# Feed-forward over quarters: the element-wise sums moved from GpSimd to VectorE, and the second product's sums read from PSUM

## The chip, the core and the metric

One core of one Trainium2 chip runs the whole program. The metric is the device time in microseconds of one execution; lower is better. The times shown are those of three runs, and one more execution was profiled.

## What is computed

One layer of a diffusion backbone over 1024 tokens of width 1024: four parallel token mixers, their gated sum and an output projection, then a feed-forward part, then a last RMSNorm. All in float32. The part that matters here is the feed-forward part and the norms around it:

```
bl = modulate(rms_norm(hl, norm_g[i, 1]), ml[3], ml[4])
hl = hl + ml[5] * (jnp.square(jax.nn.relu(bl @ w_ff1[i])) @ w_ff2[i])
return rms_norm(hl, final_g)
```

`w_ff1` is 1024 x 4096 and `w_ff2` is 4096 x 1024.

## The kernel before

The mixers take the first 948 us of the profiled execution; nothing in them is touched. The feed-forward part follows, and its order is written out by hand (`tc.manual_schedule()`): within one engine the instructions run in the order in which the Python loop emits them.

**The products.** Each of the two big products is cut into quarters (two halves of the tokens, `T1s` and `T2s`, by two halves of the contraction), and each 2 x 2 block product is made with seven products of sums and differences of quarters in place of eight products. There are 32 visits, `u` = 0 to 31: 16 for the first product, 16 for the second. A visit has seven steps, `j` = 0 to 6, so there are 224 steps. A step (`product`, lines 1469 to 1487) multiplies a 128 x 512 weight tile by one of seven stored operands `xo[j]`. Every float32 operand is held as a high part in FP32R and a low remainder, so a step is 4 x 3 = 12 matmuls of 128x512: high by high, high by low, low by high (lines 1485 to 1487). They accumulate in the PSUM banks `X`, `Y` and `Z` of the visit; the running sums of the seven-product scheme are partly made by going on accumulating in a bank after an intermediate value was read from it. Visits 0 to 9 (`PRO`) make their steps 0 and 1 first, 20 steps ahead, while the operands `xo[2]` to `xo[6]` of the second token half are still being prepared by `second_half` (lines 1619 to 1691). Visits 10 to 15 run alone; visits 16 to 31 run in pairs, step by step in turn; visits 28 to 31 make their steps 3 and 5 at the very end.

**The weights' side.** `fetch` loads four 128 x 512 quarters per visit by DMA on SP's queue, nine steps ahead at most. `weight_sum` (line 1438) makes four sums or differences of them per visit on GpSimd (line 1443), mostly in place. `prep_hi` (ScalarE, line 1461) and `prep_lo` (VectorE, through the helper `tt`, line 65) make the high part `ah` and the low part `al` of a step's weights two steps ahead; there are three buffers of each.

**After a step.** In round `n` of the main loop (from line 1900 on) these are emitted in turn: the matmuls of step `n`; `after1` or `after2` for the result of step `n - 1`; `prep_hi(n + 2)`; what was deferred to round `n` in `todo` (the weight sums among it); `prep_lo(n + 2)`; a piece of `second_half`; the fetches; and the refills.

- `after1` (line 1707), first product: ScalarE or VectorE reads the bank, the four values h11, h12, h21, h22 of the hidden layer are made, relu-squared, and turned into seven combinations. Four differences, of which two (`t3`, `t1`) go through `padd` (line 1704, GpSimd, line 1705), and the sum for h22 too. Each combination is written to DRAM (`hop`, line 1702).
- `after2` (line 1777), second product: a value is added into the residual `hl` in SBUF either by `whole`, one VectorE instruction that reads PSUM, scales and adds (line 72), or by `part`: ScalarE copies and scales the bank into an SBUF tile `m` (line 1785), and GpSimd adds `m` to `hl` a round later (line 1705).

**The refills.** The hidden combinations are the operands of the second product: from visit 15 on, the tiles `xo[j]` are loaded again from `hop`, 28 refills for each of four blocks of the contraction. A refill is a DMA load on SP's queue (line 1893), a high part on ScalarE (line 1614) and a low part on VectorE (line 1618). The main loop issues `pace` of them per round: 1.8 in the rounds before 125 and 1.35 later (line 1954). A refill's high and low parts follow its load by about four refills.

**The end.** `norm_part` squares and scales the finished pieces of `hl`, and `last_norm` totals them and scales the output (line 1869: seven instructions on VectorE and GpSimd, three of them here on GpSimd), which SP's queue stores.

Of the kernel before, what the change touches and what calls it, by code (L numbers as in the profile page):

```python
# [53 lines left out]
def tile_backbone(ctx: ExitStack, tc: tile.TileContext, a: dict, out: bass.AP):  # L54
# [9 lines left out]
    def tt(o, x, y, op):  # L64
        V.tensor_tensor(out=o, in0=x, in1=y, op=op)  # L65
# [1372 lines left out]
    def weight_sum(v, what):  # L1438

        q = v["q"]  # L1440

        def add(o, x, y, op=ALU.subtract):
            G.tensor_tensor(out=o, in0=x, in1=y, op=op)  # L1443

        if what == 4:
            q["s3"] = t_("s3", 2, where=hp)
            add(q["s3"], q[0, 0], q[1, 0])
        elif what == 3:
            add(q[1, 0], q[1, 0], q[1, 1], ALU.add)
        elif what == 2:  # L1450
            add(q[0, 0], q[1, 0], q[0, 0])
        else:
            add(q[0, 1], q[0, 1], q[0, 0])
# [156 lines left out]
    def mtile():  # L1610
        return t_("m", 4)
# [1 line left out]
    def operand_hi(j, k, src):  # L1613
        S.activation(xo[j][0][:, k], src, AF.Copy)  # L1614

    def operand_lo(j, k, src, eng=None):
        xh, xl = xo[j]
        (eng or V).tensor_tensor(out=xl[:, k], in0=src, in1=xh[:, k].bitcast(F32), op=ALU.subtract)  # L1618

    def second_half():  # L1620

        hl = box["hl"]
        y = finish_rstd(hp, box["ss"][:, :4], 4, "rf")
        dgs = hid()
        for t in range(4):
            ts(dgs[:, t * 128 : (t + 1) * 128], ident, y[:, t : t + 1], ALU.mult)
        bd = hp.tile([128, 4], F32, name="bd")
        tt(bd, modl[1][:, 4:8], modl[1][:, 0:4], ALU.subtract)
        yield
        rb = ps_n()  # L1630
        for t in range(4):
            T.matmul(rb[:, t * 128 : (t + 1) * 128], ones, dgs[:, t * 128 : (t + 1) * 128], start=True, stop=True)
        yield
        t1, t2, t3 = {}, {}, {}

        def v(k, half):
            return hl[:, k, T2s if half else T1s]

        def b2(k):
            return modl[1][:, k + 4 : k + 5]  # L1640


        def st0(k):
            second_scale(v(k, 1), k, rb)
            second_scale(v(k + 4, 1), k + 4, rb)
            t1[k] = hid()
            G.tensor_tensor(out=t1[k], in0=v(k, 1), in1=v(k, 0), op=ALU.subtract)

        def st1(k):
            second_hi(v(k + 4, 1), k + 4, xo[5])  # L1650

        def st2(k):
            operand_hi(3, k, t1[k])
            second_lo(v(k + 4, 1), k + 4, xo[5])
            t2[k] = hid()
            stt(t2[k], v(k + 4, 1), b2(k), t1[k], ALU.add, ALU.subtract)

        def st3(k):
            operand_hi(2, k, t2[k])
            operand_lo(3, k, t1[k], G)  # L1660

        def st4(k):
            operand_lo(2, k, t2[k])

            stt(t2[k], v(k + 4, 0), b2(k), t2[k], ALU.add, ALU.subtract)

        def st5(k):
            operand_hi(6, k, t2[k])

        def st6(k):  # L1670
            operand_lo(6, k, t2[k], G)

        def st7(k):
            t3[k] = hid()
            stt(t3[k], v(k + 4, 1), bd[:, k : k + 1], v(k, 1), ALU.add, ALU.subtract)

        def st8(k):
            operand_hi(4, k, t3[k])

        def st9(k):  # L1680
            operand_lo(4, k, t3[k])

        plan = {}
        for k in range(4):
            for m, f in enumerate((st0, st1, st2, st3, st4, st5, st6)):
                plan.setdefault(2 * k + m, []).append((f, k))
            for m, f in enumerate((st7, st8, st9)):
                plan.setdefault(11 + k + m, []).append((f, k))
        for n in sorted(plan):
            for f, k in reversed(plan[n]):  # L1690
                f(k)
            yield
# [8 lines left out]
    def save(j, u, x):  # L1701
        nc.sync.dma_start(hopd[j][u], x)

    def padd(o, x, y, op=ALU.add):
        G.tensor_tensor(out=o, in0=x, in1=y, op=op)  # L1705

    def after1(n, u, j, c, pro):

        if j == 0:
            c["m1"] = mtile()  # L1710
            S.activation(c["m1"], c["Z" if pro else "X"], AF.Copy)  # L1711
            if pro:
                nc.sync.dma_start(m1d[u], c["m1"])
        elif j == 1:
            h = c["h11"] = hid()
            if pro:
                square(h, c["Z"])
            else:
                tt(h, c["Z"], c["m1"], ALU.add)
                if u == 15:  # L1720
                    defer(n + 1, lambda: (square(h, h), save(0, u, h)))
                    return
                square_v(h)
            save(0, u, h)
        elif j in (2, 4):
            m = c["u2" if j == 2 else "u3"] = mtile()
            if pro:
                tt(m, c["X"], c["m1"], ALU.add)
            else:
                S.activation(m, c["X"], AF.Copy)  # L1730
            if j == 4:
                c["h22"] = hid()
                defer(n, lambda: padd(c["h22"], m, c["m5"]))
                defer(n + 1, lambda: (square(c["h22"], c["h22"]), save(5, u, c["h22"])))
        elif j == 3:
            c["m5"] = mtile()
            S.activation(c["m5"], c["Y"], AF.Copy)
            if pro:
                c["h11"] = hid()
                nc.sync.dma_start(c["h11"], hopd[0][u])  # L1740
        elif j == 5:
            h = c["h12"] = hid()
            tt(h, c["Y"], c["u2"], ALU.add)
            if pro or u == 15:
                defer(n + 1, lambda: square(h, h))
            else:
                square_v(h)

            def t3():
                t = hid()  # L1750
                padd(t, c["h22"], h, ALU.subtract)
                save(4, u, t)

            def t1():
                padd(h, h, c["h11"], ALU.subtract)
                save(3, u, h)

            def t2():
                tt(c["h22"], c["h22"], h, ALU.subtract)
                save(2, u, c["h22"])  # L1760

            def t4():
                tt(c["h21"], c["h21"], c["h22"], ALU.subtract)
                save(6, u, c["h21"])

            for k, f in enumerate((t3, t1, t2, t4)):
                defer(n + 1 + (pro or u == 15) + k, f)
        else:
            h = c["h21"] = hid()
            if pro:  # L1770
                tt(h, c["X"], c["m1"], ALU.add)
                defer(n + 1, lambda: (square(h, h), save(1, u, h)))
            else:
                square(h, c["X"])
                save(1, u, h)

    def after2(n, u, j, c):

        d = 2 * (u % 4)
        s1, s2 = modl[3][:, d : d + 1], modl[3][:, d + 1 : d + 2]  # L1780
        o11, o12, o21, o22 = (box["hl"][:, e, xs] for e in (d, d + 1) for xs in (T1s, T2s))

        def part(bank, s, o):
            m = mtile()
            S.activation(m, bank, AF.Copy, scale=s)  # L1785
            defer(n + 1, lambda: padd(o, o, m))

        def whole(bank, s, o):
            stt(o, bank, s, o, ALU.mult, ALU.add)

        last = u >= 28
        if j == 0:
            part(c["X"], s1, o11)
        elif j == 1:
            whole(c["Z"], s1, o11)
            if last:
                defer(n + 2, lambda: norm_part(n + 2, d, 0))
        elif j == 2:
            part(c["X"], s1, o12)
        elif j == 3:  # L1800
            if last:
                whole(c["Y"], s2, o22)
                norm_part(n, d + 1, 1)
            else:
                part(c["Y"], s2, o22)
        elif j == 4:
            part(c["X"], s2, o22)
        elif j == 5:
            whole(c["Y"], s1, o12)
            if last:  # L1810
                norm_part(n, d, 1)
        else:
            whole(c["X"], s2, o21)
            if last:
                norm_part(n, d + 1, 0)

    done_parts = [0, 0]
    N = len(steps)
# [90 lines left out]
    for n in range(N + 1):  # L1909
# [41 lines left out]
            S.activation(one, onec, AF.Sqrt)  # L1951
        fetch(n)
        if queue or waiting:
            pace += 1.8 if n < 125 else 1.35
            while pace >= 1.0:
                pace -= 1.0
                x = waiting.pop(0) if len(waiting) > 3 or (waiting and not queue) else None
                if queue:
                    waiting.append(queue.pop(0))
                    waiting[-1][0]()  # L1960
                if x:
                    x[1]()
                    x[2]()
                    fresh[x[3]] = (x[4], fresh[x[3]][1] + 1 if fresh[x[3]][0] == x[4] else 1)
# [84 lines left out]
```

## Time and profile before

| | us |
|---|---|
| three runs | 1612.93, 1618.04, 1617.37 |
| their median | 1617.37 |
| the profiled execution, its own time | 1611.68 |
| its span, first to last instruction | 1609.9 |
| TensorE busy in it | 1552.7 |
| VectorE busy | 1122.0 |
| ScalarE busy | 692.2 |
| GpSimd busy | 563.5 |
| first matmul of the feed-forward part starts at | 948.27 |
| last matmul of it starts at | 1588.94 |

PE is TensorE, DVE VectorE, ACT ScalarE, POOL GpSimd, SP the engine whose queue issues the DMAs. A busy time counts an instruction from its start to its end; neighbours in a pipeline overlap, so busy times can add up to a little more than the time that passed, and a 128x512 matmul of 392 ns does not mean one matmul every 392 ns. `al<-q,ah` reads: tile `al` is written from `q` and `ah`. `xl` and `xh` are the low and high parts of `xo[j]`, `m` an evacuated bank, `mm` a PSUM bank, `t` a tile of the hidden layer, `s` and `q` weight quarters.

### The profile page before, as it was taken

Reading aid. Unit: us, or ns where it says so; the run is one execution under the profiler, and the core shown is the slowest. Engines: PE = TensorE matmul, PEld = TensorE weight load, DVE = VectorE, ACT = ScalarE, POOL = GpSimd, SP = SyncE. Lnnn points to the kernel's source line nnn. Section 1 sums busy time; section 2 is a strip of 40 time slices with the busy share of each in tenths; the row PEclk is TensorE's granted clock in tenths of the full one; section 3 lists DMA queues with packets and bytes.
Section 4 is the critical chain, followed back from the end, with each engine's and each line's share of the span. In section 5 each row is a group of like instructions: output and inputs, shape, how many; then the busy total and the mean of one; then the engine's idle time right before and its main releaser. Section 6 shows DMA issues by size and latency. Waiting matters only on the chain.

```text
span 1609.9 us, 22494 instructions
## 1 busy us (share of the span) xinstructions
PE 1552.7 (96%) x8032; PEld 1277.1 (79%) x8032; DVE 1122.0 (70%) x2011; ACT 692.2 (43%) x1183; POOL 563.5 (35%) x515
## 2 busy tenths in 40 slices
PE   7999999999999999999999998999999889999996
PEld 6888878888788787778888886788888677878875
DVE  5797877975646755664443658788755969797986
ACT  3443112322336634652222346555444645554653
POOL 2311102122211111111001224687555556666673
PEclk9999999999999999999999999999999999999997
DMA  8342204335522333224233554866545644444532
GB/s 306 128 103 74 65 2 144 105 103 164 164 96 73 111 115 113 92 92 150 85 118 131 170 190 153 290 234 231 205 150 178 209 157 164 146 151 142 175 126 105
DMA packets 114080, 229.76 MB, mean 143 GB/s; under 512 B 21936, under 2 KB 27648, under 8 KB 113968
## 3 DMA queue, kind: packets, MB, share of 16 engines
q1 hardware_dynamic: 90912, 181.45, 33.4%
q0 software_dynamic: 13408, 43.49, 8.6%
q10 hardware_dynamic: 9648, 3.38, 0.9%
q8 instruction: 63, 1.03, 0.3%
q14 instruction: 49, 0.40, 0.1%
HBM read 174.56 MB, written 53.71 MB: 142 GB/s over the span
## 4 chain that ended last, share of the span: by engine, by line
PE 72%; DVE 14%; DMA 5%; issue 5%; ACT 3%; POOL 1%; SPq 0%; DVEq 0%; ACTq 0%; POOLq 0%
PE mm L79 11%; PE mm L80 11%; PE mm L81 11%; PE mm L1487 10%; PE mm L1486 9%; PE mm L1485 9%; PE po L1196 2%; DVE xl L1618 2%; DMA xl<-hop 2%; DVE al L65 2%; DMA mraw<-in_ada 1%; DMA x<-in_xT 1%; PE pt L1179 1%; PE sc L1153 1%; DVE wlo L65 1%
## 5 line engine op out<-in xcount | busy, mean ns | idle before, releaser
L1487 PE MATMUL mm<-xh,al 128*128 128x512 f32 x896 | 351.4, 392 | 9.3 <-DVE al L65 9.2
L1485 PE MATMUL mm<-xh,ah 128*128 128x512 f32 x896 | 351.1, 392 | 7.5 <-ACT m L1711 4.6
L1486 PE MATMUL mm<-xl,ah 128*128 128x512 f32 x896 | 350.5, 391 | 3.9 <-DVE xl L1618 3.9
L65 DVE TENSOR_TENSOR al<-q,ah 128x512 fp32r<-128x512 f32 x192 | 224.0, 1167 | 89.5 <-ACT ah L1461 88.9
L79 PE MATMUL mm<-alh,whi 128*128 128x512 f32 x704 | 280.1, 398 | 0.0
L81 PE MATMUL mm<-alh,wlo 128*128 128x512 f32 x704 | 276.8, 393 | 0.0
L80 PE MATMUL mm<-all,whi 128*128 128x512 f32 x704 | 276.7, 393 | 0.0
L1487 PEld LDWEIGHTS mm<-xh,al 128*128 128x128 f32 x896 | 168.8, 188 | 48.8 <-DVE al L65 13.9
L1485 PEld LDWEIGHTS mm<-xh,ah 128*128 128x128 f32 x896 | 169.0, 189 | 44.5 <-ACT m L1711 5.5
L1486 PEld LDWEIGHTS mm<-xl,ah 128*128 128x128 f32 x896 | 169.1, 189 | 41.3 <-DVE xl L1618 6.3
L1443 POOL TENSOR_TENSOR q<-q,q 128x512 f32<-128x512 f32 x104 | 158.3, 1526 | 47.5 <-DVE al L65 33.1
L1461 ACT ACTIVATE ah<-q 128x512 fp32r<-128x512 f32 x192 | 120.3, 627 | 113.6 <-PE mm L1486 88.2
L79 PEld LDWEIGHTS mm<-alh,whi 128*128 128x128 f32 x704 | 132.6, 188 | 28.0 <-issue 2.6
L81 PEld LDWEIGHTS mm<-alh,wlo 128*128 128x128 f32 x704 | 132.6, 188 | 28.0 <-issue 1.2
L80 PEld LDWEIGHTS mm<-all,whi 128*128 128x128 f32 x704 | 132.6, 188 | 27.0 <-issue 1.5
L1618 DVE TENSOR_TENSOR xl<-xl,xh 128x512 fp32r<-128x512 f32 x112 | 118.6, 1082 | 4.2 <-ACT xh L1614 4.2
L65 DVE TENSOR_TENSOR wlo<-raw,whi 128x1024 fp32r<-128x1024 f32 x60 | 75.9, 1266 | 63.5 <-ACT whi L75 52.5
L1705 POOL TENSOR_TENSOR hl<-hl,m 128x512 f32<-128x512 f32 x60 | 93.1, 1554 | 76.2 <-ACT m L1785 76.2
L1290 POOL DMA_DIRECT2D mraw<-in_ada x64 | 46.1, 721 | 205.4 <-DVE mlacc L72 92.1
L75 ACT ACTIVATE whi<-raw 128x1024 fp32r<-128x1024 f32 x44 | 46.5, 1059 | 121.0 <-PE mm L80 108.5
L1268 ACT ACTIVATE gsg<-mm 128x512 f32<-128x512 f32 x64 | 37.9, 593 | 95.2 <-PE mm L81 87.6
L72 DVE SCALAR_TENSOR_TENSOR mlacc<-mraw,sil,mlacc 128x256 f32<-128x256 f32 x112 | 54.0, 482 | 29.2 <-DMA mraw<-in_ada 27.4
(470 smaller groups left out, 2730.9 us busy)
## 6 DMA issues: line engine op xcount, KB each, us to landing
q<-in_w_ff SPq DMA_DIRECT2D x164, 256.0 KB, 4.0
hop<-t SPq DMA_DIRECT2D x112, 256.0 KB, 2.1
xl<-hop SPq DMA_DIRECT2D x112, 256.0 KB, 4.4
raw<-in_w_in SPq DMA_DIRECT2D x52, 512.0 KB, 3.6
mraw<-in_ada POOLq DMA_DIRECT2D x64, 256.0 KB, 3.5
pmd<-pm POOLq DMA_DIRECT2D x16, 512.0 KB, 3.7
pm<-pmd POOLq DMA_DIRECT2D x16, 512.0 KB, 3.9
raw<-in_w_out SPq DMA_DIRECT2D x16, 512.0 KB, 3.6
```

Source lines behind the costliest of these rows:

```text
L65: V.tensor_tensor(out=o, in0=x, in1=y, op=op)
L72: V.scalar_tensor_tensor(out=o, in0=x, scalar=s, in1=y, op0=op0, op1=op1)
L79: T.matmul(acc, w[0], x[0], start=start, stop=False)
L80: T.matmul(acc, w[0], x[1], start=False, stop=False)
L81: T.matmul(acc, w[1], x[0], start=False, stop=stop)
L1443: G.tensor_tensor(out=o, in0=x, in1=y, op=op)
L1461: S.activation(hi, v["q"][WHERE[j]], AF.Copy)
L1485: T.matmul(bank, hi[:, ks], xh[:, k], start=first and k == 0, stop=False, skip_group_check=True)
L1486: T.matmul(bank, hi[:, ks], xl[:, k], start=False, stop=False, skip_group_check=True)
L1487: T.matmul(bank, lo[:, ks], xh[:, k], start=False, stop=k == 3, skip_group_check=True)
L1618: (eng or V).tensor_tensor(out=xl[:, k], in0=src, in1=xh[:, k].bitcast(F32), op=ALU.subtract)
L1705: G.tensor_tensor(out=o, in0=x, in1=y, op=op)
```

## The change

All sums and differences of the feed-forward part that GpSimd made go to VectorE with the same operands: the weight sums, the differences in `second_half`, two of its low parts, and the differences `t1` and `t3`. In `after1` the sum for h22 reads its bank directly, with no copy `u3` ahead of it; for visits 0 to 9 the tile `m5` takes in `m1` in its place. In `after2` every value is added into `hl` by `whole`; `part` is gone. GpSimd keeps its share of the output scaling at the end. The numbers of `pace` change: 1.8 before round 124, then 1.4.

```diff
--- before.py
+++ after.py
@@ -1440,7 +1440,7 @@
         q = v["q"]
 
         def add(o, x, y, op=ALU.subtract):
-            G.tensor_tensor(out=o, in0=x, in1=y, op=op)
+            tt(o, x, y, op)
 
         if what == 4:
             q["s3"] = t_("s3", 2, where=hp)
@@ -1613,9 +1613,9 @@
     def operand_hi(j, k, src):
         S.activation(xo[j][0][:, k], src, AF.Copy)
 
-    def operand_lo(j, k, src, eng=None):
+    def operand_lo(j, k, src):
         xh, xl = xo[j]
-        (eng or V).tensor_tensor(out=xl[:, k], in0=src, in1=xh[:, k].bitcast(F32), op=ALU.subtract)
+        tt(xl[:, k], src, xh[:, k].bitcast(F32), ALU.subtract)
 
     def second_half():
 
@@ -1644,7 +1644,7 @@
             second_scale(v(k, 1), k, rb)
             second_scale(v(k + 4, 1), k + 4, rb)
             t1[k] = hid()
-            G.tensor_tensor(out=t1[k], in0=v(k, 1), in1=v(k, 0), op=ALU.subtract)
+            tt(t1[k], v(k, 1), v(k, 0), ALU.subtract)
 
         def st1(k):
             second_hi(v(k + 4, 1), k + 4, xo[5])
@@ -1657,7 +1657,7 @@
 
         def st3(k):
             operand_hi(2, k, t2[k])
-            operand_lo(3, k, t1[k], G)
+            operand_lo(3, k, t1[k])
 
         def st4(k):
             operand_lo(2, k, t2[k])
@@ -1668,7 +1668,7 @@
             operand_hi(6, k, t2[k])
 
         def st6(k):
-            operand_lo(6, k, t2[k], G)
+            operand_lo(6, k, t2[k])
 
         def st7(k):
             t3[k] = hid()
@@ -1700,9 +1700,6 @@
 
     def save(j, u, x):
         nc.sync.dma_start(hopd[j][u], x)
-
-    def padd(o, x, y, op=ALU.add):
-        G.tensor_tensor(out=o, in0=x, in1=y, op=op)
 
     def after1(n, u, j, c, pro):
 
@@ -1722,22 +1719,25 @@
                     return
                 square_v(h)
             save(0, u, h)
-        elif j in (2, 4):
-            m = c["u2" if j == 2 else "u3"] = mtile()
+        elif j == 2:
+            c["u2"] = mtile()
             if pro:
-                tt(m, c["X"], c["m1"], ALU.add)
+                tt(c["u2"], c["X"], c["m1"], ALU.add)
             else:
-                S.activation(m, c["X"], AF.Copy)
-            if j == 4:
-                c["h22"] = hid()
-                defer(n, lambda: padd(c["h22"], m, c["m5"]))
-                defer(n + 1, lambda: (square(c["h22"], c["h22"]), save(5, u, c["h22"])))
+                S.activation(c["u2"], c["X"], AF.Copy)
         elif j == 3:
+
             c["m5"] = mtile()
-            S.activation(c["m5"], c["Y"], AF.Copy)
             if pro:
+                tt(c["m5"], c["Y"], c["m1"], ALU.add)
                 c["h11"] = hid()
                 nc.sync.dma_start(c["h11"], hopd[0][u])
+            else:
+                S.activation(c["m5"], c["Y"], AF.Copy)
+        elif j == 4:
+            h22 = c["h22"] = hid()
+            tt(h22, c["X"], c["m5"], ALU.add)
+            defer(n + 1, lambda: (square(h22, h22), save(5, u, h22)))
         elif j == 5:
             h = c["h12"] = hid()
             tt(h, c["Y"], c["u2"], ALU.add)
@@ -1748,11 +1748,11 @@
 
             def t3():
                 t = hid()
-                padd(t, c["h22"], h, ALU.subtract)
+                tt(t, c["h22"], h, ALU.subtract)
                 save(4, u, t)
 
             def t1():
-                padd(h, h, c["h11"], ALU.subtract)
+                tt(h, h, c["h11"], ALU.subtract)
                 save(3, u, h)
 
             def t2():
@@ -1780,39 +1780,15 @@
         s1, s2 = modl[3][:, d : d + 1], modl[3][:, d + 1 : d + 2]
         o11, o12, o21, o22 = (box["hl"][:, e, xs] for e in (d, d + 1) for xs in (T1s, T2s))
 
-        def part(bank, s, o):
-            m = mtile()
-            S.activation(m, bank, AF.Copy, scale=s)
-            defer(n + 1, lambda: padd(o, o, m))
-
         def whole(bank, s, o):
             stt(o, bank, s, o, ALU.mult, ALU.add)
 
         last = u >= 28
-        if j == 0:
-            part(c["X"], s1, o11)
-        elif j == 1:
-            whole(c["Z"], s1, o11)
-            if last:
-                defer(n + 2, lambda: norm_part(n + 2, d, 0))
-        elif j == 2:
-            part(c["X"], s1, o12)
-        elif j == 3:
-            if last:
-                whole(c["Y"], s2, o22)
-                norm_part(n, d + 1, 1)
-            else:
-                part(c["Y"], s2, o22)
-        elif j == 4:
-            part(c["X"], s2, o22)
-        elif j == 5:
-            whole(c["Y"], s1, o12)
-            if last:
-                norm_part(n, d, 1)
-        else:
-            whole(c["X"], s2, o21)
-            if last:
-                norm_part(n, d + 1, 0)
+        bank = c["Z" if j == 1 else "Y" if j in (3, 5) else "X"]
+        col, o = {0: (s1, o11), 1: (s1, o11), 2: (s1, o12), 3: (s2, o22), 4: (s2, o22), 5: (s1, o12), 6: (s2, o21)}[j]
+        whole(bank, col, o)
+        if last and j in (1, 3, 5, 6):
+            norm_part(n, d + (j in (3, 6)), int(j in (3, 5)))
 
     done_parts = [0, 0]
     N = len(steps)
@@ -1951,7 +1927,7 @@
             S.activation(one, onec, AF.Sqrt)
         fetch(n)
         if queue or waiting:
-            pace += 1.8 if n < 125 else 1.35
+            pace += 1.8 if n < 124 else 1.4
             while pace >= 1.0:
                 pace -= 1.0
                 x = waiting.pop(0) if len(waiting) > 3 or (waiting and not queue) else None
```

## Rows read from the trace of the kernel before

**Rows 1.** The page, part 1: the span, and each engine's busy time, share and instructions.
```profile
span 1609.9 us, 22494 instructions
PE 1552.7 (96%) x8032; PEld 1277.1 (79%) x8032; DVE 1122.0 (70%) x2011; ACT 692.2 (43%) x1183; POOL 563.5 (35%) x515
```

**Rows 2.** Busy time by stretch: stretch, length, engines' busy time (instructions), clock, DMA, GB/s.
```profile
960.00:1020.00 60.00, 53.95 (x227) 43.19 (x226) 49.36 (x52) 36.89 (x66) 30.03 (x20) 0.97 0.58 194
1020.00:1060.00 40.00, 39.33 (x173) 31.80 (x172) 29.02 (x29) 20.82 (x35) 31.55 (x21) 1.00 0.76 264
1060.00:1250.00 190.00, 190.00 (x840) 157.34 (x839) 132.22 (x143) 93.08 (x159) 120.37 (x82) 1.00 0.57 197
1250.00:1320.00 70.00, 61.55 (x255) 47.92 (x254) 58.87 (x61) 39.59 (x70) 40.35 (x27) 0.98 0.54 178
1340.00:1490.00 150.00, 147.70 (x646) 120.37 (x645) 130.75 (x131) 79.04 (x137) 96.04 (x62) 1.00 0.45 151
1540.00:1560.00 20.00, 16.78 (x74) 13.58 (x73) 16.34 (x15) 9.01 (x15) 13.21 (x10) 1.00 0.41 132
```

**Rows 3.** TensorE's waits, 950 to 1610 us: total, times, longest.
```profile
PE mm L1487 <- DVE al L65: 9.2, 7, 3.2
PE mm L1485 <- ACT m L1711: 4.6, 2, 2.6
PE mm L1486 <- DVE xl L1618: 3.9, 5, 2.4
```

**Rows 4.** VectorE in order of time, 1340 to 1380 us: start, duration, instruction.
```profile
1346.58 0.68 DVE L1618 TENSOR_TENSOR xl<-xl,xh 128x512 fp32r<-128x512 f32 x1
1347.18 0.74 DVE L72 SCALAR_TENSOR_TENSOR hl<-mm,modl,hl 128x512 f32<-128x512 f32 x1
1347.84 0.68 DVE L65 TENSOR_TENSOR al<-q,ah 128x512 fp32r<-128x512 f32 x1
...
1353.06 0.74 DVE L72 SCALAR_TENSOR_TENSOR hl<-mm,modl,hl 128x512 f32<-128x512 f32 x1
...
1358.19 3.48 DVE L1618 TENSOR_TENSOR xl<-xl,xh 128x512 fp32r<-128x512 f32 x2
1361.59 1.75 DVE L65 TENSOR_TENSOR al<-q,ah 128x512 fp32r<-128x512 f32 x1
```

**Rows 5.** GpSimd in order of time, same stretch; in brackets the idle time before.
```profile
1348.66 2.23 POOL L1443 TENSOR_TENSOR q<-q,q 128x512 f32<-128x512 f32 x1 [4.42 <-DVE al L65]
...
1357.67 1.74 POOL L1705 TENSOR_TENSOR hl<-hl,m 128x512 f32<-128x512 f32 x1
1359.38 1.74 POOL L1443 TENSOR_TENSOR q<-q,q 128x512 f32<-128x512 f32 x1
1361.08 1.71 POOL L1705 TENSOR_TENSOR hl<-hl,m 128x512 f32<-128x512 f32 x1
```

**Rows 6.** Groups by line and shape, 950 to 1610 us: count, busy time, mean, idle before.
```profile
L65 DVE TENSOR_TENSOR al<-q,ah 128x512 fp32r<-128x512 f32 x188 | 220.6, 1173 | 85.8 <-ACT ah L1461 85.2
...
L1443 POOL TENSOR_TENSOR q<-q,q 128x512 f32<-128x512 f32 x104 | 158.3, 1526 | 47.5 <-DVE al L65 33.1 <-issue 7.7 <-DMA q<-in_w_ff 2.5
L1618 DVE TENSOR_TENSOR xl<-xl,xh 128x512 fp32r<-128x512 f32 x112 | 118.6, 1082 | 4.2 <-ACT xh L1614 4.2
...
L1705 POOL TENSOR_TENSOR hl<-hl,m 128x512 f32<-128x512 f32 x60 | 93.1, 1554 | 76.2 <-ACT m L1785 76.2
...
L1443 POOL TENSOR_TENSOR s<-q,q 128x512 f32<-128x512 f32 x32 | 53.6, 1676 | 10.2 <-DMA q<-in_w_ff 10.2
```

**Rows 7.** VectorE in order of time while `second_half` runs; in brackets the idle time.
```profile
968.95 0.69 DVE L65 TENSOR_TENSOR al<-q,ah 128x512 fp32r<-128x512 f32 x1 [1.77 <-ACT ah L1461]
...
977.09 0.69 DVE L65 TENSOR_TENSOR al<-q,ah 128x512 fp32r<-128x512 f32 x1 [1.10 <-ACT ah L1461]
```

**Rows 8.** ScalarE's waits, 960 to 1600 us: total, times, longest.
```profile
ACT xh L1614 <- DMA xl<-hop: 12.7, 10, 4.5
```

**Rows 9.** GpSimd's waits, 960 to 1100 us: total, times, longest.
```profile
POOL s L1443 <- DMA q<-in_w_ff: 10.2, 3, 6.1
```

## The prediction

> **What bounds the kernel now.** I read the page's first part, then busy time by stretch, then TensorE's waits, then VectorE and GpSimd in order of time. TensorE is busy for 96% of the span [rows 1], so the question is only where it is not. In the calm stretch 1060 to 1250 us it is never idle and 840 matmuls take 190.00 us [rows 2]: 0.2262 us each, 2.714 us for a step of twelve. [...] Against that rate each other stretch shows what it lost (length less matmuls times 0.2262):
>
> - 960 to 1020, while `second_half` prepares operands: 60 - 227 x 0.2262 = 8.7 us
> - 1020 to 1060: 40 - 173 x 0.2262 = 0.9
> - 1250 to 1320, the turn to the second product, refills at 1.8 per round: 70 - 255 x 0.2262 = 12.3
> - 1340 to 1490 and 1540 to 1560, refills at 1.35: 150 - 646 x 0.2262 = 3.9 and 20 - 74 x 0.2262 = 3.3 [all rows 2].
>
> That is 29.1 us, all that the change can win in front of the last matmul. The rest of the feed-forward part is matmuls back to back. What TensorE waits for in the idle gaps that the trace names is mostly VectorE: `al` 9.2 us, `xl` 3.9 us; ScalarE's `m` has 4.6 [rows 3]. VectorE is busy for 58.9 of the 70 us around the turn [rows 2].
>
> **Why VectorE is slow there.** GpSimd is idle for 4.42 us up to 1348.66 [rows 5]. In that gap VectorE starts `xl` at 1346.58, `hl` at 1347.18, `al` at 1347.84 [rows 4]: an SBUF-by-SBUF instruction of 128x512 takes 0.60 us from start to start (0.68 as listed), the one that reads PSUM 0.66 (0.74 listed). While GpSimd adds without a break, 1357.67 to 1362.79 [rows 5], two `xl` and the start of the next `al` lie 1361.59 - 1358.19 = 3.40 us apart: 1.70 each [rows 4]. The PSUM reader at 1353.06 still takes 0.74 [rows 4]. So a GpSimd addition of about 1.5 us [rows 6] makes a VectorE instruction beside it up to 1.1 us longer, which is more than the 0.60 us that the addition itself would take on VectorE.
>
> **The change, part by part.** Added to VectorE: 136 weight sums (104 + 32, rows 6), 32 hidden differences (two for each of 16 visits) and 12 pieces of `second_half`, 180 x 0.60 = 108 us; 60 sums into `hl` [rows 6] as `whole`, 60 x 0.66 = 40 us; 16 sums for h22 from PSUM, 11 us at 0.66 (the `m5` of visits 0 to 9 takes the place of their `u3`, so nothing is left over there). Together 159 us. Taken away: 188 `al` go from 1.173 to 0.60, 108 us; 112 `xl` from 1.082 to 0.60, 54 us [rows 6]; together 162 before the smaller groups. VectorE's total does not grow. What counts is the load of a step, 2.714 us:
>
> - **Refills at 1.4 a round:** `al` 0.60, sums 136/224 x 0.60 = 0.36, `whole` 0.66, refills 1.4 x 0.60 = 0.84: 2.46 us. It fits. Before, contended, two `xl` and one `al` alone are 5.1 us where GpSimd is busy, 1.8 us where it is not.
> - **Refills at 1.8:** 0.60 + 0.36 + 0.66 + 1.08 = 2.70 us. It just fits, with no room to catch up.
> - **`second_half`:** its heaviest pair of steps holds 11 VectorE pieces and two `al`, 2 x 0.66 + 0.60 + 0.66 + 0.66 + 0.60 + 0.66 + 0.60, an odd step's 0.60, and 1.20: 6.9 us for 5.43. So it still overruns, for two or three pairs. Now a pair lasts 977.09 - 968.95 = 8.1 us [rows 7]; I take 7.3 for then, the 6.9 and 0.4 of idling: ScalarE stays a link between the two steps, for whose `ah` VectorE now idles 1.77 and 1.10 us [rows 7].
>
> What moves or waits anew:
>
> - The sums now stand in VectorE's one queue, ahead of `prep_lo` and the refills. A sum that waits for its weights holds those. GpSimd's waits for weights were 10.2 us in 3 times [rows 9] and 2.5 in one [rows 6], out of 136. Those three lie ahead of 1100, where GpSimd's queue carries them without much harm: 1020 to 1060 lost 0.9. On VectorE the `al` are made a step ahead, which covers 2.7 us. I cost it at 0, bound 3.4 above (6.1 - 2.7), nothing below.
> - `whole` waits for the matmuls of step `n - 1`, and behind it stand `al(n+2)` and the refills' low parts. The `al` is wanted 2.7 us later and is done 1.6 us after that end (0.66 + 0.36 + 0.60). Cost 0; if the cover is gone, TensorE waits for `al`.
> - The banks: X is read by VectorE in place of ScalarE and continued a step (visits alone) or three steps (pairs) later. Cost 0 by the same 0.66 us.
> - ScalarE loses 60 copies, which stand ahead of `ah` in its queue, so `ah` comes no later. SP's queue issues the same loads and stores; fetches wait for buffers that `al` frees, so they come earlier. GpSimd has no DMA here. The new `pace` shortens a block of 28 refills from 21 rounds to 20: 0.
>
> The sum: 960 to 1020 keeps 3.7 of 8.7 (two pairs, each 1.9 over, are 3.8): gain 5.0, bounds 0 and 8.7. 1020 to 1060 is a matter of DMAs: 0. 1250 to 1320 keeps a quarter: ScalarE's refills waited 12.7 us for DMAs [rows 8], and the load has no room; gain 9, bounds 0 and 12.3. The later refills keep 0.7 of 7.2: gain 6.5, bounds 0 and 7.2. From the last matmul to the end nothing is costed; its output scaling keeps its GpSimd part, the bounds are 1 us either way. Gain 20.5 us against the profiled execution's 1611.7: 1591.2. The median of the runs stands 5.7 above that execution (1617.4), so I say **1597**.
>
> **Duration or distance.** The sum uses the distance of starts, 0.60, not the 0.68 listed [rows 4]. With 0.69 and 0.74 a step is 2.82 us at 1.4 and 3.09 at 1.8: over by 0.11 in 60 rounds and 0.37 in 16, 6.4 and 6.0 us; the gain would be about 10.
>
> [...]
>
> **The rivals.**
>
> 1. *Distance 0.60, VectorE relieved* (forecast): 1597, with its own range 1590 to 1604. Chance 0.55.
> 2. *VectorE full at 0.69 an instruction.* Against it: the 0.60 between starts, though that is one gap of 4.4 us [rows 4]. For it: waits that I have not seen add up in one queue. 1611.7 - 10 + 5.7 = 1607. Chance 0.16.
> 3. *The turn belongs to the DMAs.* ScalarE waits for `hop` loads, 4.5 us at the longest [rows 8]. If the turn's 12.3 us stay, the gain is 11.5: 1606. Chance 0.14.
> 4. *It comes to the same.* VectorE's waits for ScalarE's `ah` are 85 us now [rows 6]; if such a wait leaves 0.27 us a round unused in the 76 refill rounds, the 20.5 are gone: 1613 to 1618. Chance 0.08.
> 5. *Slower: sums that wait for weights.* Place: the sum of `s` at the head of a visit, on VectorE. Price: the longest wait now, 6.1, less the 2.7 of cover, 3.4 us each. It decides from six such waits (20.5); at one for each of the ten pairs and the twos at the end, 34 us, the time is 1617 + 14 = 1631. Against it: 4 waits in 136, three of them ahead of 1100 [rows 6, 9]. Chance 0.07.
>
> That the change does not do what it says I exclude: no addition of this part is left on GpSimd in the diff.
>
> **How the numbers follow.** Cases 1 to 3 are faster by more than 0.3% (4.9 us, about what a measurement of this kernel can tell from no change), less a little at their upper edge: 0.84. Same 0.09, slower 0.07. The range must hold cases 1 to 3: below, all 29 us gone at the usual level is 1588, and a gain of 25 in a run near the profiled level 1587, which I take. Above, 1612, the edge of no change, which leaves out cases 4 and 5 and little else.
>
> **What would show it.** In the profile after: GpSimd busy for under 10 us behind 950; every `al` and `xl` near 0.68; VectorE's busy time behind 950 not above the old; the stretch of the turn with few waits on `xl` and `al`; waits left around `second_half`. Wrong if VectorE's starts lie 0.69 apart, if VectorE waits for `q<-in_w_ff` in many visits, or if the turn shows long waits on `hop`.

## The result, and the profile after

The changed kernel takes 1592.13 us in the median of four runs (1588.19 to 1592.78) beside 1615.77 for the kernel before (1612.93 to 1618.04): a ratio of 0.984, 95% interval 0.983 to 0.986. The forecast was 1597 in a range of 1587 to 1612.

The page of the changed kernel, part 1, answers to [rows 1]:

```profile
span 1589.8 us, 22190 instructions
PE 1542.6 (97%) x8032; PEld 1272.3 (80%) x8032; DVE 1109.3 (70%) x2267; ACT 649.8 (41%) x1107; POOL 168.5 (11%) x259
```

VectorE has 256 instructions more and is busy 13 us less. Busy time by stretch of the changed kernel, to be read beside [rows 2]; the columns are the same:

```profile
960.00:1020.00 60.00, 58.26 (x255) 47.26 (x254) 48.83 (x77) 40.56 (x71) 0.00 (x0) 1.00 0.65 219
1020.00:1060.00 40.00, 39.20 (x174) 32.14 (x173) 31.80 (x52) 18.67 (x32) 0.00 (x0) 1.00 0.75 256
1060.00:1250.00 190.00, 190.00 (x840) 157.39 (x839) 140.17 (x221) 89.14 (x152) 0.00 (x0) 1.00 0.57 198
1250.00:1320.00 70.00, 66.20 (x288) 53.23 (x287) 60.48 (x97) 34.79 (x62) 0.00 (x0) 1.00 0.61 203
...
1340.00:1490.00 150.00, 150.00 (x664) 124.24 (x663) 125.36 (x198) 63.90 (x112) 0.00 (x0) 1.00 0.43 146
```

At 0.2262 us a matmul, 960 to 1020 now loses 60 - 255 x 0.2262 = 2.3 us (8.7 before), 1020 to 1060 loses 0.6 (0.9), the turn 4.9 (12.3), 1340 to 1490 nothing (3.9). The 3.3 lost between 1540 and 1560 are gone too: TensorE is busy for all 20.00 us there. The granted clock of the first stretch went from 0.97 to 1.00. TensorE's waits from 945 to 1590 us, to be read beside [rows 3]:

```profile
PE pn L242 <- DVE t L65: 3.2, 1, 3.2
PE mm L1485 <- ACT xh L1614: 2.5, 1, 2.5
...
PE mm L1487 <- DVE al L65: 1.5, 2, 0.9
PE mm L1485 <- ACT m L1708: 0.9, 2, 0.4
...
PE mm L1486 <- DVE xl L65: 0.6, 2, 0.4
```

`al` has fallen from 9.2 to 1.5 us, `m` from 4.6 to 0.9, `xl` from 3.9 to 0.6. Within the products one wait of 2.5 us for a refill's high part is the largest now; the 3.2 us ahead of `pn`, a matmul of the last norm, are the same in the kernel before. VectorE in order of time during the later refills, beside [rows 4]:

```profile
1340.70 0.74 DVE L72 SCALAR_TENSOR_TENSOR hl<-mm,modl,hl 128x512 f32<-128x512 f32 x1
1341.37 0.68 DVE L65 TENSOR_TENSOR q<-q,q 128x512 f32<-128x512 f32 x1
1341.96 0.68 DVE L65 TENSOR_TENSOR al<-q,ah 128x512 fp32r<-128x512 f32 x1
1342.57 0.68 DVE L65 TENSOR_TENSOR xl<-xl,xh 128x512 fp32r<-128x512 f32 x1
1343.17 0.74 DVE L72 SCALAR_TENSOR_TENSOR hl<-mm,modl,hl 128x512 f32<-128x512 f32 x1
```

Sum, low parts and `whole` follow each other 0.60 and 0.66 us apart, and the work of this round, with one sum and one refill, is over in 1343.17 - 1340.70 = 2.47 us, in front of the next step's 2.71. The groups of 945 to 1590 us, beside [rows 6], say the same of all of them (0.688 for 1.173, 0.683 for 1.082):

```profile
L65 DVE TENSOR_TENSOR al<-q,ah 128x512 fp32r<-128x512 f32 x192 | 132.0, 688 | 33.1 <-ACT ah L1461 32.9
...
L65 DVE TENSOR_TENSOR xl<-xl,xh 128x512 fp32r<-128x512 f32 x112 | 73.7, 683 | 7.6 <-ACT xh L1614 7.6
```

A measure that leaves the mixers out is the time from the start of the first `ah` matmul of the feed-forward part to that of the last, from the view of line 1485. The first row is the kernel before, the second the changed one; behind the durations stand the first and the last start:

```profile
L1485 PE MATMUL mm<-xh,ah x896: 387/389/632, 943.8 to 1588.5; 128*128 128x512 f32 x180
```
```profile
L1485 PE MATMUL mm<-xh,ah x896: 388/389/503, 946.9 to 1570.1; 128*128 128x512 f32 x180
```

That is 644.7 us before and 623.2 after: 21.5 less. (The 948.27 in the table of the kernel before is the second step's start, not the first's.) The mixers, which did not change, took 943.8 us in the one and 946.9 in the other. Below, this length stands beside each experiment's time, since it comes from one execution but holds only the part in question. It ends at the last start of line 1485 and leaves out the last norm behind it.

### The profile page after: what moved, and what is told of

The parts are those of the page before. It is cut to its first block, busy times and chain, and to the rows that moved or that the text cites. A ratio compares the mean times of both kernels' runs of the same rounds, so it can differ in the third digit from the quotient of the medians.

```text
span 1589.8 us, 22190 instructions
## 1 busy us (share of the span) xinstructions
PE 1542.6 (97%) x8032; PEld 1272.3 (80%) x8032; DVE 1109.3 (70%) x2267; ACT 649.8 (41%) x1107; POOL 168.5 (11%) x259
## 4 chain that ended last, share of the span: by engine, by line
PE 73%; DVE 11%; issue 7%; DMA 5%; ACT 3%; POOL 1%; SPq 0%; DVEq 0%; ACTq 0%; POOLq 0%
PE mm L1486 11%; PE mm L1485 11%; PE mm L1487 11%; PE mm L79 9%; PE mm L80 9%; PE mm L81 9%; PE po L1196 2%; DMA mraw<-in_ada 1%; DMA x<-in_xT 1%; PE pt L1179 1%; DVE wlo L65 1%; PE sc L1153 1%; PE sc L1154 1%; DVE s5ta L65 1%; DMA hl<-hld 1%
## 5 line engine op out<-in xcount | busy, mean ns | idle before, releaser
L65 DVE TENSOR_TENSOR al<-q,ah 128x512 fp32r<-128x512 f32 x192 | 132.0, 688 | 33.1 <-ACT ah L1461 32.9
L72 DVE SCALAR_TENSOR_TENSOR hl<-mm,modl,hl 128x512 f32<-128x512 f32 x112 | 83.7, 747 | 40.0 <-PE mm L1487 40.0
L65 DVE TENSOR_TENSOR xl<-xl,xh 128x512 fp32r<-128x512 f32 x112 | 73.7, 683 | 7.6 <-ACT xh L1614 7.6
L1845 POOL TENSOR_TENSOR hl<-hl,t 128x1024 f32<-128x1024 f32 x3 | 7.6, 2548 | 630.8 <-ACT t L1840 630.8
L1614 ACT ACTIVATE xh<-xl 128x512 fp32r<-128x512 f32 x112 | 66.4, 618 | 14.9 <-DMA xl<-hop 14.8
```

Source lines behind the costliest of these rows:

```text
L72: V.scalar_tensor_tensor(out=o, in0=x, scalar=s, in1=y, op0=op0, op1=op1)
```

## The experiments

Each is an edit of the changed kernel. Times are medians, with the ratio to the kernel before run beside them; "length" is that of the feed-forward part in the profiled execution.

| kernel | us | ratio (95%) | length, us |
|---|---|---|---|
| before | 1615.77 | 1 | 644.7 |
| changed | 1592.13 | 0.984 (0.983 to 0.986) | 623.2 |
| changed, once more | 1594.19 | 0.986 (0.984 to 0.988) | 623.0 |
| idle additions on GpSimd | 1608.87 | 0.996 (0.994 to 0.997) | 641.1 |
| weight sums back | 1594.66 | 0.987 (0.985 to 0.989) | 623.4 |
| second product's sums back | 1595.99 | 0.987 (0.986 to 0.989) | 627.4 |
| both back | 1607.02 | 0.994 (0.992 to 0.996) | 635.9 |
| `second_half` back | 1601.06 | 0.990 (0.988 to 0.992) | 629.4 |
| one more VectorE addition a round | 1603.51 | 0.993 (0.991 to 0.994) | 633.2 |
| ScalarE's copies kept | 1593.74 | 0.988 (0.986 to 0.989) | 623.8 |
| old pace | 1592.72 | 0.986 (0.985 to 0.988) | 622.2 |
| stores of visit 15 on GpSimd's queue | 1591.22 | 0.985 (0.984 to 0.987) | 619.7 |
| the same, once more | 1588.35 | 0.983 (0.981 to 0.985) | 619.8 |

**Is it GpSimd beside VectorE, or GpSimd's late results?**

```diff
+        if v["u"] >= 16:
+            src = {4: q.get("s3"), 3: q.get((1, 0)), 2: q.get((0, 0)), 5: q.get((0, 1))}[what]
+            G.tensor_tensor(out=t_("m", 4), in0=src, in1=src, op=ALU.add)
```

> The changed kernel with 72 additions of 128x512 put on GpSimd for the weight sums of visits 16 to 31; each reads a finished sum and writes a spare tile that nobody reads. Theory A (GpSimd beside VectorE makes VectorE's instructions longer, by up to 1.1 us for each): a round of the refills then has 2.46 + 0.64 x 1.1 = 3.17 us of VectorE work at 1.4 and 3.40 at 1.8, for a step of 2.71, so 60 x 0.45 + 14 x 0.69 = 37 us at most are lost: 1605 to 1628 us, and al and xl rise from 0.69 to over 0.9 us in the mean. Theory B (GpSimd delivered its own results late, nothing else): these results are read by nobody, so 1592 within 3 us.

1608.87 us, length 641.1: 17.9 us more for 72 results that nobody reads, and no engine's waits in this trace name them. Theory A holds, B falls: the mere running of GpSimd's additions costs most of what the change had gained. That late results cost nothing beside it in the kernel before is not shown by this. VectorE and then GpSimd of this kernel in order of time:

```profile
1360.29 0.68 DVE L65 TENSOR_TENSOR al<-q,ah 128x512 fp32r<-128x512 f32 x1
1360.89 1.52 DVE L65 TENSOR_TENSOR xl<-xl,xh 128x512 fp32r<-128x512 f32 x1
1362.34 0.74 DVE L72 SCALAR_TENSOR_TENSOR hl<-mm,modl,hl 128x512 f32<-128x512 f32 x1
```
```profile
1360.51 1.36 POOL L1456 TENSOR_TENSOR m<-q 128x512 f32<-128x512 f32 x1 [2.55 <-DVE q L65]
```

The `xl` that starts while GpSimd adds takes 1.52 us and ends at 1362.41, 0.54 us behind the addition (1360.51 + 1.36 = 1361.87). It was the same before: the `al` of [rows 4] ends 0.55 us behind the addition of [rows 5] at 1362.79. In this trace 41 VectorE instructions of 128x512 with their inputs in SBUF alone start during one of GpSimd's additions, and 39 of them end 0.5 to 0.6 us behind it. So the VectorE instruction is not longer by one factor throughout: it ends about half a microsecond behind the addition, and what an addition costs VectorE depends on when it falls. In the mean `al` rises only to 0.755 and `xl` to 0.885, so these two groups lose 190 x 0.067 + 112 x 0.202 = 35 us over 72 additions: 0.49 us each, not the 1.1 at most. That the mean of `al` would pass 0.9 was wrong.

**Which part carries the gain?**

```diff
-            tt(o, x, y, op)
+            G.tensor_tensor(out=o, in0=x, in1=y, op=op)
```

in `weight_sum` alone:

> The changed kernel with the 136 weight sums back on GpSimd and everything else as changed. Theory A: VectorE saves 0.36 us a round and loses 0.61 x 1.1 = 0.67: 2.77 at 1.4 and 3.01 at 1.8, 60 x 0.06 + 16 x 0.30 = 8 us lost: 1596 to 1602 us. Theory C (VectorE's load is what counts, relieve it): 136 x 0.60 = 82 us less work on VectorE, 1587 to 1591 us. Theory B: sums come at 1.5 us each in place of 0.6, some us slower, but with al and xl at 0.69.

Length 623.4, the same as the changed kernel's within 0.2 us; the median, 1594.66 us, is 0.5 us above that of the changed kernel's second set of runs, and the single runs of the two overlap. No theory hit. VectorE has 136 instructions less, and `al` from `q` takes 0.836, `xl` 0.827: 192 x 0.148 + 112 x 0.144 = 45 us longer. The groups `al` from `s` (32 at 1.004, 0.683 in the changed kernel) and `t` from `t` (76 at 0.864 for 0.704) add 10 and 12, small ones 3: 70 us, 0.51 per addition. That is a little less than the 0.60 that a sum takes on VectorE, so with everything else moved already the move of these relieves nothing. Then the second product's sums alone, where `part` (copy on ScalarE, addition on GpSimd) came back:

```diff
+        def part(bank, s, o):
+            m = mtile()
+            S.activation(m, bank, AF.Copy, scale=s)
+            defer(n + 1, lambda: G.tensor_tensor(out=o, in0=o, in1=m, op=ALU.add))
...
-        whole(bank, col, o)
+            part(c["X"], s1, o11)
...
```

> The changed kernel with the old way of the second product's sums alone: 60 copies on ScalarE and 60 additions on GpSimd. Theory A: 60 x (1.1 - 0.66) = 26 us more of VectorE time over 112 rounds, 0.24 a round: 2.70 at 1.4 (just fits) and 2.94 at 1.8 (16 x 0.22 = 3.5 lost): 1594 to 1600 us. Theory C: 40 us less on VectorE, 1588 to 1592 us.

1595.99 us and a length of 627.4, 4.2 more: inside A's range. And the two edits together:

> The changed kernel with both the weight sums (136) and the second product's 60 copies and additions back on GpSimd and ScalarE. Alone these cost 0.2 and 4.2 us from the first to the last step. Theory F (a full VectorE: nothing is lost until the load of a round passes the step): 1.14 GpSimd additions a round, 0.60 + 0.84 + 0.31 + 1.26 = 3.0 us at 1.4 against 2.71, so 10 to 16 us slower, 1602 to 1608 us. Theory G (each part costs its own): the two add up, 4 to 5 us slower, 1595 to 1598 us.

1607.02 us, length 635.9: 12.7 us more, where the parts alone make 0.2 + 4.2 = 4.4. Theory F's number holds and G falls: the parts do not add up. F's reason, that VectorE is full, is not what its busy time shows. Two stretches of this kernel:

```profile
1250.00:1320.00 70.00, 64.32 (x269) 50.75 (x268) 58.11 (x65) 40.27 (x71) 37.29 (x24) 0.98 0.59 193
1340.00:1490.00 150.00, 147.82 (x646) 120.53 (x646) 131.10 (x133) 78.58 (x138) 96.85 (x61) 1.00 0.45 150
```

The later refills lose 150 - 646 x 0.2262 = 3.9 us again, as in [rows 2] of the kernel before, with the same 646 matmuls; the turn loses 9.2. VectorE is busy for only 131.1 of those 150 us, as it was before (130.75), so it is late in single rounds and not full over the stretch; which rounds make the loss was not told apart. The third part is `second_half`, its four differences and eight low parts back on GpSimd:

```diff
-            tt(t1[k], v(k, 1), v(k, 0), ALU.subtract)
+            G.tensor_tensor(out=t1[k], in0=v(k, 1), in1=v(k, 0), op=ALU.subtract)
...
-            operand_lo(3, k, t1[k])
+            operand_lo(3, k, t1[k], G)
...
-            operand_lo(6, k, t2[k])
+            operand_lo(6, k, t2[k], G)
```

> The changed kernel with only the 12 pieces of second_half back on GpSimd (four differences, eight low parts). The stretch 960 to 1020 lost 8.7 us before and 2.3 after. Theory A (these 12 make it, by running beside VectorE and by being late for it): the loss comes back, 5 to 7 us slower, 1597 to 1599 us. Rival: the weight sums that stood among them made it, then 0 to 2 us slower.

1601.06 us, length 629.4: 6.2 us more from 12 instructions. The time is above the range of theory A; beside the changed kernel's 1594.19 of the same set of runs it is 6.9 us more, inside its 5 to 7. The stretch, then VectorE and GpSimd in it:

```profile
960.00:1020.00 60.00, 54.50 (x234) 44.01 (x234) 46.15 (x58) 39.23 (x69) 17.54 (x12) 0.97 0.53 170
```
```profile
976.84 1.42 DVE L72 SCALAR_TENSOR_TENSOR xl<-hl,modl,xh 128x512 fp32r<-128x512 f32 x1
978.18 1.78 DVE L72 SCALAR_TENSOR_TENSOR t<-hl,modl,t 128x512 f32<-128x512 f32 x1
```
```profile
976.41 1.31 POOL L1647 TENSOR_TENSOR t<-hl 128x512 f32<-128x512 f32 x1 [4.41 <-DVE hl L72]
977.66 1.76 POOL L1618 TENSOR_TENSOR xl<-t,xh 128x512 fp32r<-128x512 f32 x1
```

It loses 60 - 234 x 0.2262 = 7.1 us, and its clock is back at 0.97. The two VectorE instructions behind the scaling take 1.42 and 1.78 where the changed kernel has 0.74 for each, the first beside the difference `t` (976.41 to 977.72), the second beside a low part (977.66 to 979.42); each ends 0.54 us behind GpSimd's instruction. How much of the 6.2 comes from this and how much from the low parts that GpSimd delivers late was not told apart. The three parts, 12.7 and 6.2, make 18.9 of the 21.5; the hidden layer's 48 sums and the rest were not tried alone.

**Is VectorE's load of a round the bound?**

```diff
+            if n > 112:
+                tt(mtile(), box["hl"][:, 0, T1s], box["hl"][:, 0, T1s], ALU.add)
```

> The changed kernel with one more addition of 128x512 in SBUF on VectorE in each round after 112 that has refills, some 70 to 80 of them; it reads a piece of the residual and writes a spare tile that nobody reads. If VectorE's load of a round is what bounds the refills, at 0.60 us an instruction: 3.06 us at 1.4 and 3.30 at 1.8 against 2.71, 60 x 0.35 + 11 x 0.58 = 27 us at most, 1607 to 1620 us. If VectorE has room (its busy share is 83% there) or the DMAs set the pace: 1592 to 1596 us.

1603.51 us, length 633.2: 10 us more, between the two. This and the changed kernel from 1320 to 1540 us:

```profile
1320.00:1540.00 220.00, 216.44 (x945) 175.99 (x943) 216.72 (x352) 99.01 (x171) 0.00 (x0) 1.00 0.47 154
```
```profile
1320.00:1540.00 220.00, 220.00 (x972) 182.25 (x971) 185.79 (x293) 101.11 (x174) 0.00 (x0) 1.00 0.46 155
```

VectorE is full (216.7 of 220) and TensorE loses 220 - 945 x 0.2262 = 6.2 us there, none in the changed kernel; the turn loses 8.3 for 4.9. But 27 us were forecast for the upper case. A block of refills has 28 steps, 76.0 us, and only 20 rounds with refills: 20 x 3.06 + 8 x (2.46 - 0.84) = 74.2 us of VectorE work. It fits over the block; what falls behind in the refill rounds is made good in the others, and only what a refill's due step can't wait for is lost. That reading is worked out, not tried by itself.

**ScalarE's relief and the pace.** The copies kept, read by nobody:

```diff
+            if j in (0, 2, 4) or (j == 3 and u < 28):
+                S.activation(mtile(), bank, AF.Copy, scale=s)
```

> The changed kernel with the 60 scaled copies of the second product kept on ScalarE; nobody reads them. If ScalarE's relief was part of the gain, ah comes about 0.6 us later and the time rises by 3 us or more, 1595 us and above. Theory A: 1592 within 2 us.

1593.74 us, length 623.8: 0.6 us. And the old numbers of the refills:

```diff
-            pace += 1.8 if n < 124 else 1.4
+            pace += 1.8 if n < 125 else 1.35
```

> The changed kernel with the old numbers of pace (1.8 before round 125, then 1.35). Costed at nothing: 1592 within 2 us. If the new numbers brought some of the gain: 1594 us or more.

1592.72 us, length 622.2. Neither is part of the gain.

**What the turn still loses.** SP's queue in the changed kernel; start, time from the first to the last issue, what is issued:

```profile
1268.59 0.32 SPq L1702 DMA_DIRECT2D hop<-t  x1
1269.00 0.88 SPq L1869 DMA_DIRECT2D xl<-hop  x2
1272.26 0.32 SPq L1702 DMA_DIRECT2D hop<-t  x1
1272.67 0.89 SPq L1869 DMA_DIRECT2D xl<-hop  x2
```

Two refill loads follow each store, and the stores of visit 15 wait for VectorE's differences, one in each round. So:

```diff
     def save(j, u, x):
-        nc.sync.dma_start(hopd[j][u], x)
+        (G if u == 15 else nc.sync).dma_start(hopd[j][u], x)
```

> The changed kernel with the seven stores of visit 15 to DRAM on GpSimd's DMA queue in place of SP's. The turn to the second product still loses 4.9 us, and TensorE's one long wait there is for a refill whose load left SP's queue at 1279. Theory D (the loads stand in SP's queue behind stores that wait for VectorE's differences): the loads leave earlier, 2 to 4.5 us faster, 1587.5 to 1590 us. Theory E (the transfers themselves take the time): 1592 within 1.5 us.

The length fell to 619.7, 3.5 us less, but the median, 1591.22, is above D's range. In the profiled execution, the slowest of its four, the mixers took 950.2 us. So it ran once more beside the changed kernel:

> The changed kernel once more, for comparison with the runs beside it: 1592 us, ratio 0.984.

> The changed kernel with the seven stores of visit 15 on GpSimd's DMA queue once more, beside the changed kernel. From the first step to the last it took 619.7 us in place of 623.2, but its mixers took 3.3 us longer in that one execution. If the gain is real and the mixers only vary from run to run: 3 us faster than the changed kernel, 1589 us. If the stores on GpSimd's queue cost elsewhere: the same, 1592.

1588.35 us (1586.58 to 1592.76) beside 1594.19 (1593.46 to 1594.29), length 619.8 beside 623.0. SP's queue and the turn in it, one kernel:

```profile
1246.01 11.29 SPq L1869 DMA_DIRECT2D xl<-hop  x16
1257.65 17.07 SPq L1436 DMA_DIRECT2D q<-in_w_ff  x6
```
```profile
1250.00:1320.00 70.00, 68.93 (x302) 56.04 (x301) 62.53 (x102) 35.61 (x63) 3.25 (x6) 1.00 0.57 197
```

Sixteen loads leave in a row, and the turn loses 70 - 302 x 0.2262 = 1.7 us in place of 4.9. ScalarE's waits for `xl<-hop` fell there from 13.7 us in the changed kernel beside it to 2.1. Theory D's mechanism holds: 3.2 to 3.5 us of the length are its work. But the length leaves out the last norm, and that took longer: from the last start of line 1485 to the end of the span it was 19.7 and 20.1 us in the two profiles of the changed kernel and 21.7 in both with the stores moved. The difference lies in sixteen small matmuls, here in the changed kernel and then with the stores moved:

```profile
1574.10 1.92 PE L242 MATMUL pn<-ones,t 128*128 128x1 f32 x16 [3.20 <-DVE t L65]
```
```profile
1568.78 3.54 PE L242 MATMUL pn<-ones,t 128*128 128x1 f32 x16 [3.19 <-DVE t L65]
```

Behind the same wait the granted clock of the four us from their start is 0.73 in the one and 0.50 in the other. So from the first `ah` matmul to the end of the span only 1.4 to 1.7 us are left (642.9 and 643.1 against 641.4 and 641.5). Whether the moved stores bring the lower clock was not tried; in the changed kernel with the old pace the 32 matmuls `pn<-ones,t` average the same 298 ns as with the stores moved (247 in the changed kernel). The rest of the 5.8 between the medians is not explained: the intervals of the two ratios still touch (0.981 to 0.985 and 0.984 to 0.988). All four runs of this version lie below the four of the changed kernel beside them, so it is probably the fastest of all, by how much is open.

## Why the prediction was right

The gain forecast was 20.5 us, on a profiled span of 1609.9; the span after is 1589.8, and the feed-forward part is 21.5 us shorter. That the span fell by 20.1 is in part luck: 21.5 us came from the part and 1.7 from the end behind it, and the untouched mixers happened to take 3.1 more. The mechanism is the one that was forecast, and the steps missed in both directions:

- *960 to 1020*: 5.0 forecast of 8.7, 6.4 measured. The heaviest pair of steps was taken as 7.3 us (its sum has nine pieces and two `al`; the "11 VectorE pieces and two `al`" counts these two twice). In the changed kernel's VectorE a pair of ten instructions lasts 7.0 us, 970.91 to 977.94, and the heaviest, with eleven, 7.7, to 985.63. That is 1.6 and 2.3 over two steps, but TensorE lost only 2.3 in all, so not every overrun reached it:

```profile
970.91 0.69 DVE L65 TENSOR_TENSOR al<-q,ah 128x512 fp32r<-128x512 f32 x1 [1.17 <-ACT ah L1461]
...
977.94 0.69 DVE L65 TENSOR_TENSOR al<-q,ah 128x512 fp32r<-128x512 f32 x1 [0.50 <-ACT ah L1461]
...
985.63 0.69 DVE L65 TENSOR_TENSOR al<-q,ah 128x512 fp32r<-128x512 f32 x1 [0.56 <-ACT ah L1461]
```

- *The turn*: 9 forecast, 7.4 measured. The step "the turn keeps a quarter" was too small: it kept 4.9 of 12.3. Its reason was named, ScalarE's wait for `hop`, but as a matter of the transfers (third rival); the stores run showed that the order of SP's queue made most of it (1.7 us lost in place of 4.9).
- *Later refills*: 6.5 forecast, 7.2 measured, all that there was.
- *Sums that wait for weights*: cost 0. VectorE waited once, 2.7 us. The fifth rival, one such wait in every pair, did not come:

```profile
DVE s L65 <- DMA q<-in_w_ff: 2.7, 1, 2.7
```

- *Distance 0.60*: it held with sums, low parts and `whole` in one queue. The 2.47 us of the round shown is no measurement of the 2.46 forecast: that is a mean with 0.61 sums and 1.4 refills, the round shown has one of each, and the two only happen to add up alike. The second rival did not come: the starts lie 0.60 apart at a duration of 0.68. (That case's gain of "about 10" is 20.5 - 12.4 = 8.1 by its own terms.)
- *After the last matmul*: 0 forecast, within 1 us either way. From the last start of line 1485 to the end of the span it was 21.4 us before and is 19.7, so 1.7 are outside those bounds. The sixteen matmuls shown above at 1.92 us took 3.55 in the kernel before, at a granted clock of 0.50:

```profile
1592.52 3.55 PE L242 MATMUL pn<-ones,t 128*128 128x1 f32 x16 [3.20 <-DVE t L65]
```

- *The level*: the step that failed is the last one, adding 5.7 us because the median of three runs stood that far above the profiled execution (with the fourth run it is 4.1). The changed kernel's profiled execution, 1592.04, lay at its median. That is the 5 us between 1597 and 1592. The profiled execution of the kernel before, 1611.68, lay below all of its timed runs; the last section shows what varies.

One reason holds only in part: that an addition on GpSimd costs VectorE more than the 0.60 it takes there. Taken over all of VectorE's 128x512 groups (count times what the mean is above the changed kernel's), the kernel before lost 173 us by 256 additions, 0.67 each. With both groups back it is 136 us by 196, 0.69; with the second product's sums alone 47 by 60, 0.78; with the weight sums alone 0.51. So what a part of the move brings depends on what GpSimd still does: from the kernel with both groups back, moving the weight sums alone shortens the length from 635.9 to 627.4, but with the other sums moved already it brings nothing (623.4 to 623.2).

One sum mixed two measures: the 162 us taken away set listed durations (1.173 and 1.082) against the distance of starts, 0.60. With durations on both sides (0.688 and 0.683) `al` and `xl` give 91 + 45 = 136, and the rest of the 173 came from the smaller groups that the prediction left out.

## What to carry to other kernels

Look at what an engine's instruction costs its neighbour, not only at its own time: compare the same instruction's duration where the other engine runs and where it is idle, in all groups and not in the two largest alone. Sum the load of the in-order queue by round against the bound engine's step, with the distance between starts and not the listed duration, and then over a whole block: here one more addition a round cost 10 us where the sum by round gave 27, by the author's estimate because VectorE caught up in the rounds without refills. Parts of such a change need not add up: here the weight sums put back cost 0.2 us of length, the second product's sums 4.2, and both together 12.7.

## What was not expected

The untouched mixers ended anywhere from 943.8 to 950.2 us in the thirteen profiled executions, a spread of 6.4 us, while the feed-forward part repeated within 0.2 us (623.2 and 623.0 for the changed kernel, 619.7 and 619.8 with the stores moved). For a change to the late part its length in one profile tells more than a median of four runs, if the end behind it is counted too: that took 19.7 to 21.7 us, longest, 21.4 to 21.7, in the five where the last norm's 32 matmuls `pn<-ones,t` averaged 298 ns in place of the changed kernel's 247. And 72 additions whose results nobody reads cost 17.9 us of it, nearly as much as all 256 that the change removed.
